# A hybrid attention and mixture-of-experts layer on one core: TensorE's other work within an attention step dealt in three parts instead of two

## The chip, the cores and the metric

One core of a Trainium2 chip runs the whole layer as one program. The metric is the device time of one execution in microseconds (us): here the median of three runs of the kernel before.

## The reference

512 tokens of width 1024, one layer, all in float32. What the attention part computes:

```python
h = rms_norm(x, g_mix)
qa, ka, va, qb, kb, vb, qi, ki, wi, ga, gb = split(h @ w_in)      # 8 heads of 64 for a and b, 8 for the indexer
o_a = softmax(mask_a(rope(qa) rope(ka).T / 8)) @ va               # branch a: block-sparse, causal
score = sum_h wi * relu(rope(qi) . rope(ki))                      # indexer: the 128 best keys of each query
o_b = softmax(mask_topk(rope(qb) rope(kb).T / 8)) @ vb            # branch b: only those keys
x = x + (sigmoid(ga) * (o_a @ w_proj_a) + sigmoid(gb) * (o_b @ w_proj_b)) @ w_out
x = x + hier_moe(rms_norm(x, g_ffn))                              # top group of 4, then 2 of its 8 experts
return rms_norm(x, g_final)
```

## The kernel before, in words

The program has three parts in time. It normalises and transposes x and projects the first chunks of columns; it runs the attention, with the rest of the input projections dealt between its steps; then it applies the output projection, routes the tokens and runs all 32 experts, whose weights come in 192 pieces of 1024 KB.

**Weights of the projections.** Each chunk of 256 columns comes by DMA from SP's queue into `raw` buffers (three of them). ScalarE casts each half to the matmul's format (`split`, line 169: the high part, `wh`), and VectorE (first half) or GpSimd (second half) subtracts it from the raw value (line 170: the low part, `wl`). A projection is a row of groups of three 128x512 matmuls (lines 255 to 257: high by high, high by low, low by high), each group an item of the generator `proj_T`.

**The attention.** `attend(quad, work)` is called for a0, a1, b0 and b1, four heads each. A quad has eight steps: two pairs of heads by four query tiles i of 128 rows, with (i+1)*128 keys each. A step has three pieces.

- `scores`: for each of the two heads two matmuls into one of two score banks (lines 432, 433); VectorE adds the mask and takes the minimum (436), ScalarE takes the exponential (437), VectorE the reciprocal and the scaling (438, 439) into `e`.
- `transposes`: TensorE turns `e` by 128x128 blocks (448), and ScalarE copies the result from PSUM to `pt` (450), one copy for each of the two heads.
- `values`: TensorE multiplies `pt` with v (460). At a pair's last tile ScalarE and VectorE split the result into two parts (464, 465).

Transposes and values are those of the step before the scores'. Between the pieces TensorE is given `work`: the generator `others()`, which holds the remaining projections, the indexer's scores (389, 390, with ScalarE's 391 and VectorE's 393), the gates (line 487 is their tanh on ScalarE) and the merge of branch a (503 to 505). `run(work, cost)` takes items from it until their costs (0.64 for a group of three matmuls) use up the amount due. `SHARE` gives for each quad the amount ahead of its first scores and the amount in a step. What is left over is run behind the quad by `run_to`.

VectorE also carries the search for the top keys (`topk`, lines 402 to 404), which is queued behind a0 and runs on through a1 into b0. The order of TensorE's instructions is the program's own in this part (`manual_schedule`), while a scheduler orders those of the other engines around it. [...]

Of the kernel before, what the change touches and what calls it, by code (L numbers as in the profile page):

```python
# [136 lines left out]
def layer_kernel(ctx: ExitStack, tc: tile.TileContext, xT, x, w_ki, w_ch, w_ab, w_out, g_mix, g_ffnk, g_fin, w_r, b_r,  # L137
# [20 lines left out]
    def t2(shape, dtype=F32, name="t2", tag="r"):  # L158
        return temps[tag][0].tile(shape, dtype, tag=tag, name=name, bufs=temps[tag][1])

    def small(shape, name, dtype=F32):
        return sm.tile(shape, dtype, tag=name, name=name)
# [99 lines left out]
    def run(gen, cost=1e9):  # L262

        due[0] += cost
        while due[0] > 0:
            c = next(gen, None)
            if c is None:
                due[0] = 0.0
            elif isinstance(c, str):
                done.add(c)  # L270
            else:
                due[0] -= c
# [142 lines left out]
    def attend(quad, work):  # L415

        br, n4 = quad[0], int(quad[1])
        qs, (ks, klo), v = Q[quad], K[quad], V[br]
        bias_of = causal if br == "a" else sparse
        oh, ol = oT[br]  # L420
        steps = [(pr, i) for pr in range(2) for i in range(NT)]
        es, pts, ops = {}, {}, {}

        def scores(pr, i):
            n = (i + 1) * P
            nm = max(n, 2 * P)
            es[pr, i] = []
            for s in range(2):
                j = 2 * pr + s
                ps = pa.tile([P, 512], F32, tag="sc", name="ps")  # L430
                q = qs[:, j, i * P:(i + 1) * P]
                pe.matmul(ps[:, :nm], q, ks[:, j, :nm], start=True, stop=False)
                pe.matmul(ps[:, :nm], q, klo[:, j, :nm], start=False, stop=True)
                e = t2([P, T], name="e", tag="e")
                st = small([P, 3], "st")
                dve.tensor_tensor_reduce(e[:, :n], ps[:, :n], bias_of(i), -0.125, 3e38, ALU.add, ALU.min, st[:, 0:1])  # L436
                act.activation(ps[:, :n], e[:, :n], AF.Exp, bias=st[:, 0:1], scale=-1.0, accum_out=st[:, 1:2])  # L437
                dve.reciprocal(st[:, 2:3], st[:, 1:2])
                dve.tensor_scalar(e[:, :n], ps[:, :n], st[:, 2:3], None, ALU.mult)
                es[pr, i].append(e)  # L440

        def transposes(pr, i):
            n = (i + 1) * P
            pts[pr, i] = []
            for e in es.pop((pr, i)):
                tr = pt_.tile([P, 512], F32, tag="tr", name="tr")
                for kt in range(i + 1):
                    pe.transpose(tr[:, kt * P:(kt + 1) * P], e[:, kt * P:(kt + 1) * P], ident)
                pt = t2([P, T], name="pt", tag="p")
                act.copy(pt[:, :n], tr[:, :n])  # L450
                pts[pr, i].append(pt)

        def values(pr, i):
            if i == 0:
                ops[pr] = pb.tile([P, 512], F32, tag="o", name="ops")
            pt = pts.pop((pr, i))
            for kt in range(i + 1):
                for s in range(2):
                    h = 4 * n4 + 2 * pr + s
                    pe.matmul(ops[pr][64 * s:64 * s + 64, i * P:(i + 1) * P], v[:, kt, h * DH:(h + 1) * DH],  # L460
                              pt[s][:, kt * P:(kt + 1) * P], start=kt == 0, stop=kt == i)
            if i == NT - 1:
                o = ops.pop(pr)
                act.copy(oh[:, 2 * n4 + pr], o)
                dve.tensor_tensor(ol[:, 2 * n4 + pr], o, oh[:, 2 * n4 + pr].bitcast(F32), ALU.subtract)

        first, share = SHARE[quad]
        run(work, first)
        for m in range(len(steps) + 1):
            if m < len(steps):  # L470
                scores(*steps[m])
            run(work, share / 2)
            if m > 0:
                transposes(*steps[m - 1])
            run(work, share / 2)
            if m > 0:
                values(*steps[m - 1])
        S.free(qs, ks, klo)


# [69 lines left out]
    def others():  # L550
        yield from qk("qi0")
        yield from together(qk("qi1", "qa1", "ka1"), idx_scores(), RATIO)
        yield "a1"
        yield from v_proj("vb")
        yield from qk("qb0", "kb0")
        yield "b0"
        yield from merge_a()
        S.free(*oT["a"])
        yield from qk("qb1", "kb1")
        yield "b1"  # L560
        yield from gates_b()
        yield "end"

    run(v_proj("va"))
    oT["a"] = pair_of_outputs()
    work = others()
    attend("a0", work)
    run_to(work, "a1")
    attend("a1", work)
    S.free(V["a"])  # L570
    run_to(work, "b0")
    oT["b"] = pair_of_outputs()
    for i in range(1, NT):
        topk(i)
    attend("b0", work)
    x2 = []

# [46 lines left out]
    for n in range(4):  # L624
# [6 lines left out]
        for b in range(2):  # L631
# [9 lines left out]
            m = ma[c // 4][:, c % 4]  # L641
# [500 lines left out]
```

## Time and profile before

| what | value |
|---|---|
| median of three runs | 941.35 us (941.22 to 945.83) |
| the profiled execution | 942.32 us; its span 940.4 us |
| TensorE matmuls (PE) | busy 875.7 us, 93% of the span |
| VectorE (DVE) | busy 433.8 us, 46% |
| ScalarE (ACT) | busy 278.3 us, 30% |
| GpSimd (POOL) | busy 176.5 us, 19% |
| mean granted clock of TensorE | 0.985 of full speed |
| HBM traffic | 241.33 MB read, 259 GB/s over the span |

The span is the profiled execution from its first to its last recorded instruction; the execution's own time is 1.9 us longer. The shares are means over stages with different limits: the attention runs from 66 to 372.6 us of the span, the output projection and the routing follow, and from about 470 us on the expert weights flow. A time in a timeline is counted from the start of the span.

### The profile page before, as it was taken

How to read it: one execution, taken by the hardware profiler on the slowest of the kernel's cores; microseconds unless marked ns; L12 is line 12 of the kernel's file. 1: busy time of each engine (PE TensorE's matmuls, PEld its weight loads, DVE VectorE, ACT ScalarE, POOL GpSimd, SP SyncE). 2: the span in 40 equal slices, each digit the busy share in tenths (PEclk: the TensorE clock that was granted, in tenths of full speed). 3: DMA queues.
4: the chain of work that ended last, by engine and by line, in shares of the span. 5: the costliest groups of instructions: out<-in, count | busy, mean ns of one | idle time of the engine just before them, and what ended most of it. 6: DMA issues, size and time to landing. Idle time of an engine off the chain costs nothing. (4 is left out here: it accounts for less than half of the span.)

```text
span 940.4 us, 15614 instructions
## 1 busy us (share of the span) xinstructions
PE 875.7 (93%) x6436; PEld 517.1 (55%) x6436; DVE 433.8 (46%) x991; ACT 278.3 (30%) x585; POOL 176.5 (19%) x112
## 2 busy tenths in 40 slices
PE   7999999989999999889999999998998989987885
PEld 5897779768777877689834342422423223232221
DVE  4737899998544545941823322231322212213004
ACT  5546654562444544433501000000100000100004
POOL 2495334342214711221200000000000000000003
PEclk9999999999999999899999999999999999999898
DMA  8422112112224223455679999999999999999985
GB/s 330 157 71 67 55 36 90 48 57 77 77 82 180 87 69 112 135 229 228 226 317 421 419 420 421 420 418 422 419 420 420 421 422 419 421 420 419 402 327 217
DMA packets 41118, 244.51 MB, mean 260 GB/s; under 512 B 4944, under 2 KB 5328, under 8 KB 16336
## 3 DMA queue, kind: packets, MB, share of 16 engines
q1 hardware_dynamic: 41040, 243.45, 65.0%
q8 instruction: 52, 0.85, 0.4%
q14 instruction: 26, 0.21, 0.1%
HBM read 241.33 MB, written 2.10 MB: 259 GB/s over the span
## 5 line engine op out<-in xcount | busy, mean ns | idle before, releaser
L860 PE MATMUL h<-we,xs 128*32 128x512 f32 x2048 | 238.4, 601 | 26.3 <-DMA we<-in_w_e_dram 19.4
L860 PEld LDWEIGHTS h<-we,xs 128*32 128x32 f32 x2048 | 59.1, 110 | 180.5 <-issue 117.4
L867 PE MATMUL y<-we,hT 128*32 128x512 f32 x1024 | 116.3, 595 | 5.3 <-DMA we<-in_w_e_dram 5.2
L255 PE MATMUL mm<-xh,wh 128*128 128x512 f32 x272 | 109.9, 404 | 0.8 <-DVE bias L393 0.8
L257 PE MATMUL mm<-xh,wl 128*128 128x512 f32 x272 | 107.5, 395 | 0.0
L256 PE MATMUL mm<-xl,wh 128*128 128x512 f32 x272 | 107.5, 395 | 0.0
L1072 POOL TENSOR_TENSOR fo<-x,gfn 128x512 f32<-128x512 f32 x4 | 5.0, 1282 | 450.0 <-DVE x L927 450.0
L170 POOL TENSOR_TENSOR wl<-raw,wh 128x1024 fp32r<-128x1024 f32 (+1 forms) x23 | 64.5, 2803 | 132.1 <-ACT wh L169 68.5
L927 DVE TENSOR_TENSOR x<-cps,x 128x512 f32<-128x512 f32 x64 | 43.3, 688 | 86.3 <-PE cps L925 86.1
L867 PEld LDWEIGHTS y<-we,hT 128*32 128x32 f32 x1024 | 30.0, 109 | 77.1 <-issue 57.0
L901 DVE SCALAR_TENSOR_TENSOR silu<-silu,gate,h 128x512 f32<-128x512 f32 x16 | 12.0, 747 | 124.5 <-issue 82.8
L257 PEld LDWEIGHTS mm<-xh,wl 128*128 128x128 f32 x272 | 51.1, 188 | 12.6 <-DVE wl L170 0.4
L255 PEld LDWEIGHTS mm<-xh,wh 128*128 128x128 f32 x272 | 51.1, 188 | 11.7 <-issue 1.2
L256 PEld LDWEIGHTS mm<-xl,wh 128*128 128x128 f32 x272 | 51.2, 188 | 9.5
L169 ACT CAST wh<-raw 128x1024 fp32r<-128x1024 f32 (+1 forms) x46 | 45.6, 1028 | 31.9 <-DMA raw<-in_w_ch_dram 13.5
L169 ACT CAST y<-y 128x512 fp32r<-128x512 f32 x32 | 18.8, 586 | 121.7 <-PE y L867 121.7
L908 ACT COPY hT<-htr 128x512 f32<-128x512 f32 x16 | 8.7, 589 | 150.2 <-PE htr L906 150.2
L895 ACT ACTIVATE silu<-h 128x512 f32<-128x512 f32 x16 | 9.6, 598 | 145.1 <-PE h L860 145.1
L170 DVE TENSOR_TENSOR y<-y,y 128x512 fp32r<-128x512 f32 x32 | 22.0, 689 | 62.9 <-ACT y L169 62.8
L437 ACT ACTIVATE ps<-e,st 128x128 f32<-128x128 f32 (+3 forms) x64 | 33.5, 524 | 43.9 <-DVE st L436 43.6
L170 DVE TENSOR_TENSOR wl<-raw,wh 128x1024 fp32r<-128x1024 f32 (+1 forms) x23 | 31.9, 1389 | 26.9 <-ACT wh L169 22.3
L677 PE MATMUL mm<-woh,mt 128*128 128x256 f32 x128 | 37.4, 293 | 0.0
(201 smaller groups left out, 1570.7 us busy)
## 6 DMA issues: line engine op xcount, KB each, us to landing
we<-in_w_e_dram SPq DMA_DIRECT2D x192, 1024.0 KB, 19.8
raw<-in_w_ch_dram SPq DMA_DIRECT2D x44, 512.0 KB, 4.1
raw<-in_w_ab_dram SPq DMA_DIRECT2D x8, 512.0 KB, 4.1
raw<-in_w_out_dram SPq DMA_DIRECT2D x6, 512.0 KB, 4.2
xraw<-in_xT_dram SPq DMA_DIRECT2D x8, 256.0 KB, 5.8
xtok<-in_x_dram SPq DMA_DIRECT2D x4, 512.0 KB, 9.1
x<-in_x_dram SPq DMA_DIRECT2D x4, 512.0 KB, 5.1
out_dram<-fo SPq DMA_DIRECT2D x8, 256.0 KB, 2.3
```

Of the source, the lines that this page charges most:

```text
L169: act.copy(hi, raw)
L170: eng.tensor_tensor(lo, raw, hi.bitcast(F32), ALU.subtract)
L255: pe.matmul(ps, a, xk(k, 0), start=k == 0, stop=False)
L256: pe.matmul(ps, a, xk(k, 1), start=False, stop=False)
L257: pe.matmul(ps, lo[:, k, col:col + P], xk(k, 0), start=False, stop=k == NK - 1)
L437: act.activation(ps[:, :n], e[:, :n], AF.Exp, bias=st[:, 0:1], scale=-1.0, accum_out=st[:, 1:2])
L677: pe.matmul(ps, a, hi[:, k], start=k == 0, stop=False)
L860: pe.matmul(ps[h][CAP * e:CAP * (e + 1)], xs[:, k, h, CAP * e:CAP * (e + 1)], w[:, e * FF:(e + 1) * FF], start=k == 0, stop=k == NK - 1)
L867: pe.matmul(ys[h][CAP * e:CAP * (e + 1)], hT[h][:, k, CAP * e:CAP * (e + 1)], w[:, e * FF:(e + 1) * FF], start=k == 0, stop=k == 3)
L895: act.activation(out[h], h1[h], AF.Silu)
L901: dve.scalar_tensor_tensor(a[h], a[h], gate[:, h:h + 1], h3[h], ALU.mult, ALU.mult)
L927: dve.tensor_tensor(o, ps, o, ALU.add)
```

## The change

In `attend` the work between two scores was dealt in halves: one between the scores and the transposes, one between the transposes and the values. Now it is dealt in thirds, and the last third follows the values. In the ninth round of a quad, which has no scores, the last third isn't run there: it is left to what follows the quad. Two lines longer, the program has every line behind 476 two higher.

```diff
@@ -469,12 +469,14 @@
         for m in range(len(steps) + 1):
             if m < len(steps):
                 scores(*steps[m])
-            run(work, share / 2)
+            run(work, share / 3)
             if m > 0:
                 transposes(*steps[m - 1])
-            run(work, share / 2)
+            run(work, share / 3)
             if m > 0:
                 values(*steps[m - 1])
+            if m < len(steps):
+                run(work, share / 3)
         S.free(qs, ks, klo)
```

**TensorE at the first values of b1.** `tr` is the bank of the transposes, `ops` the accumulator of the values, `mm` that of a projection. Before, nine matmuls of work stand between transposes and values, the last six of which are the first six rows here:

```order
L255 MATMUL mm<-xh_96,wh 128x512
L256 MATMUL mm<-xl_98,wh 128x512
L257 MATMUL mm<-xh_96,wl 128x512
L255 MATMUL mm<-xh_97,wh 128x512
L256 MATMUL mm<-xl_99,wh 128x512
L257 MATMUL mm<-xh_97,wl 128x512
L460 MATMUL ops<-pt,vb_1339 64x128 x2
L432 MATMUL ps<-hikb_35_2999,qb_32_2902 128x384
L433 MATMUL ps<-lokb_36_3000,qb_32_2902 128x384
```

Now:

```order
L460 MATMUL ops<-pt,vb_1349 64x128 x2
L255 MATMUL mm<-xh_96,wh 128x512
L256 MATMUL mm<-xl_98,wh 128x512
L257 MATMUL mm<-xh_96,wl 128x512
L255 MATMUL mm<-xh_97,wh 128x512
L256 MATMUL mm<-xl_99,wh 128x512
L257 MATMUL mm<-xh_97,wl 128x512
L432 MATMUL ps<-hikb_35_2999,qb_34_2918 128x384
L433 MATMUL ps<-lokb_36_3000,qb_34_2918 128x384
```

The values (line 460) moved ahead of six matmuls of work, which now stand between them and the next scores (432).

**ScalarE at the first two steps of b1.** Line 487 is 489 in the changed kernel. Before:

```order
L437 ACTIVATE ps,st<-e,st 128x256
L169 CAST wh<-raw 128x1024 x2
L437 ACTIVATE ps,st<-e,st 128x256
L487 ACTIVATE g<-g 128x512
L450 COPY pt<-tr 128x128 x2
L437 ACTIVATE ps,st<-e,st 128x384 x2
```

Now:

```order
L437 ACTIVATE ps,st<-e,st 128x256
L169 CAST wh<-raw 128x1024 x2
L437 ACTIVATE ps,st<-e,st 128x256
L450 COPY pt<-tr 128x128
L489 ACTIVATE g<-g 128x512
L450 COPY pt<-tr 128x128
L437 ACTIVATE ps,st<-e,st 128x384 x2
```

The tanh of a gate moved from ahead of both copies (450) to between them; the two casts (169) stay ahead of the second exponential.

**ScalarE at the second step of b0.** `wab` is a weight of branch a's output. Before:

```order
L169 CAST wh<-raw 128x1024 x2
L437 ACTIVATE ps,st<-e,st 128x384 x2
L169 CAST wab<-raw 128x1024
L450 COPY pt<-tr 128x256 x2
L487 ACTIVATE g<-g 128x512
```

Now:

```order
L169 CAST wh<-raw 128x1024
L437 ACTIVATE ps,st<-e,st 128x384
L169 CAST wh<-raw 128x1024
L437 ACTIVATE ps,st<-e,st 128x384
L169 CAST wab<-raw 128x1024
L450 COPY pt<-tr 128x256 x2
L489 ACTIVATE g<-g 128x512
```

One of the two exponentials (437) moved in between the two casts of `wh`; the copies still stand behind the cast of `wab`.

## Rows read from the trace of the kernel before

**Rows 1.** Each stretch: start:end, length, busy us by engine, clock, DMA share, GB/s.

```profile
66.00:148.80 82.80, 78.21 (x476) 63.94 (x476) 71.41 (x187) 48.70 (x106) 40.60 (x25) 1.00 0.20 66
148.80:223.00 74.20, 68.76 (x419) 56.02 (x418) 71.73 (x184) 36.93 (x80) 28.14 (x18) 1.00 0.19 64
223.00:317.40 94.40, 94.40 (x487) 74.96 (x486) 50.89 (x116) 41.31 (x82) 29.97 (x14) 1.00 0.29 101
317.40:372.60 55.20, 55.20 (x319) 43.41 (x318) 26.85 (x76) 27.61 (x65) 10.84 (x7) 1.00 0.26 80
...
470.00:926.00 456.00, 423.56 (x3722) 143.75 (x3714) 115.17 (x195) 39.16 (x71) 5.00 (x4) 0.99 0.99 407
```

**Rows 2.** Waits of PE up to 470 us: total us, times, longest us.

```profile
PE ps L432 <- DVE e L439: 5.4, 4, 2.1
PE ips L389 <- DVE bias L393: 3.0, 5, 1.3
```

**Rows 3.** Line 450 (copies): what ended ScalarE's idle time, who waited for them (us, times).

```profile
  PE tr L448: 25.8, 23
  PEld ops L460: 1.1, 3
```

**Rows 4.** Timelines of PE, ACT, PE, b1: a group of work, the last copies and values.

```profile
322.63 0.39 PE L255 MATMUL mm<-xh,wh 128*128 128x512 f32 x1
323.33 0.40 PE L255 MATMUL mm<-xh,wh 128*128 128x512 f32 x1
...
367.05 1.07 ACT L450 COPY pt<-tr 128x512 f32<-128x512 f32 x2 [1.53 <-PE tr L448]
369.43 1.09 PE L460 MATMUL ops<-pt,vb 128*64 128x128 f32 x16
```

**Rows 5.** Timeline of ACT, then of PE, the last values of a1.

```profile
200.98 0.62 ACT L316 CAST hikb<-r 64x512 fp32r<-64x512 f32 x1 [2.86 <-DVE r L285]
...
203.42 1.06 ACT L450 COPY pt<-tr 128x512 f32<-128x512 f32 x2
204.25 1.37 PE L460 MATMUL ops<-pt,va 128*64 128x128 f32 x16
```

**Rows 6.** Timeline of ACT, then of PE, the second values of b0.

```profile
241.74 1.05 ACT L169 CAST wh<-raw 128x1024 fp32r<-128x1024 f32 x1 [1.75 <-DMA raw<-in_w_ch_dram]
...
243.30 0.56 ACT L437 ACTIVATE ps<-e,st 128x384 f32<-128x384 f32 x1
...
244.85 0.63 ACT L450 COPY pt<-tr 128x256 f32<-128x256 f32 x2
247.11 0.66 PE L460 MATMUL ops<-pt,vb 128*64 128x128 f32 x8
```

**Rows 7.** Timeline of ACT, then of PE, the fourth values of b0.

```profile
263.02 1.05 ACT L169 CAST wh<-raw 128x1024 fp32r<-128x1024 f32 x1 [1.73 <-DMA raw<-in_w_ch_dram]
265.13 1.09 PE L460 MATMUL ops<-pt,vb 128*64 128x128 f32 x16
```

**Rows 8.** Timeline of ACT, then of PE, the first values of b1.

```profile
326.02 0.62 ACT L487 ACTIVATE g<-g 128x512 f32<-128x512 f32 x1
326.55 0.41 ACT L450 COPY pt<-tr 128x128 f32<-128x128 f32 x2
327.14 0.44 PE L460 MATMUL ops<-pt,vb 128*64 128x128 f32 x4
```

**Rows 9.** Timelines of POOL, DVE (two places) and PE, second scores of a1.

```profile
150.58 2.40 POOL L170 TENSOR_TENSOR wl<-raw,wh 128x1024 fp32r<-128x1024 f32 x1 [0.37 <-POOL loka L319]
151.05 3.01 DVE L170 TENSOR_TENSOR wl<-raw,wh 128x1024 fp32r<-128x1024 f32 x1
...
186.92 1.21 DVE L170 TENSOR_TENSOR wl<-raw,wh 128x1024 fp32r<-128x1024 f32 x1
155.59 0.35 PE L432 MATMUL ps<-hika,qa 128*128 128x256 f32 x1 [1.82 <-DVE e L439]
```

**Rows 10.** Timeline of SP's queue, after the attention.

```profile
409.36 2.60 SPq L609 DMA_DIRECT2D we<-in_w_e_dram  x5
```


## Prediction

> **What bounds the kernel now.** I read the stretches first, because the attention and what follows it have different limits. [...] From 470 on the DMA engines are 0.99 busy: there the expert weights set the pace.
>
> Second, the waits of TensorE [rows 2]: the score matmul of line 432 waits 4 times for line 439 (VectorE's scaling of an earlier step, which frees the score bank), 5.4 us in all and at most 2.1; the indexer's matmul of line 389 waits 3.0 us in 5 pieces. Third, the copies, the operation between transposes and values: [rows 3] shows that only 1.1 us, in 3 places and on the weight load alone, was ever waited for them. The time from the transposes to the values covers them.
>
> Does a delay in the attention reach the end? The burst of expert weights is issued from 409.36 on [rows 10], behind the attention and the output projection, and from there transfers fill the rest [rows 1]. So I pass a delay of TensorE on one to one (an estimate: nothing in 372 to 470 moves against the attention's end).
>
> **The change part by part.** No instruction is added or dropped: the same matmuls stand in another order, and VectorE's and ScalarE's orders are made anew around it; SP's and GpSimd's stay as they were. A group of three 128x512 matmuls takes 0.70 us (322.63 to 323.33, [rows 4]). One step of b1 had 2.10 us of such work on either side of the transposes; now it has 1.40 before them, 1.40 behind them and 1.40 behind the values. Two consequences:
>
> *Scores to scores.* The distance between a step's scores and the next is the same, so the waits for line 439 [rows 2] stay: 0. What a value matmul frees (the pt buffers, the accumulator) nobody waits for.
>
> *Transposes and values come sooner.* The transposes of step m-1 need the exponentials that the scores of step m already needed, by way of the banks: no wait there, 0. The values need ScalarE's copies, and the cover of the copies shrinks by a third. In an ordinary step of b1 the two copies start at 367.05, as soon as the transposes let them, and take 1.07, while the values start at 369.43 [rows 4]: 1.31 us behind the copies' end. With 0.70 less work between, a cushion of 0.6 is left, and a step waits only where ScalarE has something else ahead of the copies. I went through all 32 steps for that, and three places are left.
>
> *a1's last values.* Before, from the last scores to these values lay 7.0 us of other work, now 5.6, so they are due 1.40 earlier, at 202.85 instead of 204.25. But ScalarE works in order, and four casts of the key stack stand ahead of the two copies both before and now: they begin at 200.98, when VectorE's r is ready, 0.62 each, and the copies run from 203.42 to 204.48 [rows 5]. Already before, the values ran 1.37 us instead of 1.09 ([rows 5] against [rows 7], both of 16 matmuls), held by the second copy. They end no sooner now, with 1.40 us more work left behind them: +1.4 at most, 0 if r comes earlier by as much. VectorE carries two instructions fewer ahead of r there, so I take +1.1, near the top.
>
> *b0's second values.* Due 247.11 - 2 x 1.40 = 244.3. The copies stood behind a cast whose DMA landed at 241.74 and ended at 244.85 + 0.63 = 245.48 [rows 6], 1.2 later. Now one exponential of 0.56 more runs ahead of that cast, so the copies may end at 244.9: +0.6 to +1.2, and 0 if the transfer lands sooner; I take +0.8.
>
> *b0's fourth values.* The copies stood behind a cast that waited for its transfer until 263.02, and the values followed at 265.13 [rows 7]. Now the copies stand ahead of that cast in ScalarE's order: 0. Were they still behind it, the values, due 4.2 us of work behind the scores where it was 6.3, would wait those 2.1.
>
> *b1's first values.* Due 327.14 - 1.40 = 325.74. Two casts, an exponential and the gate's tanh (0.62) stand ahead of the copies, which ended at 326.55 + 0.41 = 326.96 [rows 8]. The new order puts the tanh between the two copies: the last one still ends near 327.0. +1.3, bounds 0 and 1.5.
>
> *a0.* TensorE rests 82.80 - 78.21 = 4.6 us there, waiting for VectorE [rows 1, 2], and small waits for copies would run beside that; the indexer's waits can move a little either way: 0, bounds -0.5 and +0.5.
>
> *The third that falls away at a quad's last step* runs behind the last values instead, unbroken, for the same time: 0. *DMA issues and GpSimd's subtractions*: their order is the same, and the buffers are freed by the same matmuls at the same count of work: 0. *Clock*: in both a stretches the granted clock stayed 1.00 in spite of waits of up to 2.1 us [rows 1, 2], and the new ones are shorter: 0.
>
> Sum: 0 + 1.1 + 0.8 + 0 + 1.3 = **+3.2 us**. The profiled execution took 942.32 us (span 940.4), so 945.52; the median of the runs is 0.97 lower, hence **944.6 us**.
>
> **The rivals.**
>
> *1. The port race of a1's second step flips: 942.8.* VectorE's subtraction of line 170 at 151.05 took 3.01 us where the same at 186.92 took 1.21, and GpSimd's half of the same chunk ran from 150.58 to 152.98 [rows 9]; behind it stood the scalings for which the scores at 155.59 waited 1.82. So 3.01 - 1.21 = 1.80 us belong to who came first. In the new order VectorE has two of the search's instructions fewer ahead of this subtraction and could start at about 150.5, just ahead of GpSimd: then GpSimd is late (nobody waits for it) and the wait goes: 944.6 - 1.8. For it: the order; against: the margin is under 0.2 us. [...]
>
> *2. Slower: ScalarE's order costs a wait at many steps: 947.8.* The cushion of an ordinary step of b1 is 0.6 us (taken for a1 too), one tanh is 0.62 [rows 8] and one cast 1.05 [rows 7]. If a cast slips ahead of the copies at about half of the 14 other steps of these two quads, each waits 1.05 - 0.6 = 0.45: 7 x 0.45 = 3.2 on top of the 3.2: 945.52 + 3.2 - 0.97. It decides at the point where something on ScalarE holds the copies up by more than the 0.6. For it: ScalarE's order changed at several places, and VectorE's products that gate the tanh move against the copies. Against: ScalarE sat idle for the transposes 23 times in the 32 steps [rows 3], so there nothing stood ahead. [...]
>
> *3. It does nothing: 941.4.* The r of a1, the transfer of b0 and the tanh of b1 all come as much earlier as the values. For it: they hang on TensorE's work, in part. Against: the casts wait for transfers.
>
> *4. Faster: the scores' 5.4 us [rows 2] go as well and no new wait comes: 942.32 - 5.4 - 0.97 = 936.0.* Against: VectorE is busy 71.73 of 74.20 us in a1 [rows 1], which leaves 2.5 to win there.
>
> **How the numbers follow.** The forecast gets 0.43, rival 1 0.20, rival 2 0.20, rival 3 0.13, rival 4 0.04. A measurement of this kernel can tell about 0.5%, 4.7 us, from no change: 936.6 to 946.1. Rival 4 is faster (0.04). Rival 2 and the upper bounds of the forecast (0.5 + 1.4 + 1.2 + 2.1 + 1.5 = 6.7, 948.0) are slower: 0.20 + 0.04 = 0.24. All else, 0.72, is the same. The low end is the port race with all terms near their lows (942.32 - 1.8 + 0.4 - 0.97 = 940.0), the high end rival 2: 940.0 to 947.8. That leaves out rival 4 and the tails of rivals 1 and 2, under 0.2.
>
> **What would show it.** Right: in the waits, the copies of line 450 appear with about 3 us on line 460, in a1's end, b0's second and b1's first step, and line 432 keeps some 5 us; TensorE's busy time is unchanged, and the burst of expert weights starts about 3 us later. Rival 1: the subtraction at about 151 takes 1.2, and line 432's waits fall to 3.6. Rival 2: waits for line 450 at more than six steps. Rival 3: none of over 0.3. I am wrong in kind if TensorE's waits in the attention change by less than a microsecond but the burst's start moves, or if the time differs with the burst unmoved: then the end does not hang on the attention as I say.

## The result, and the profile after

The changed kernel takes **951.15 us** (median of 5 runs, 950.77 to 951.2) against 941.35 (5 runs, 938.27 to 945.83): a ratio of 1.0099, interval 1.0073 to 1.0125. It is slower by 9.8 us, where 944.6 was forecast with a range up to 947.8.

Where the time went is read first by stretches, as [rows 1] of before. In the changed kernel (start and end, length, busy us by engine, granted clock, DMA share, GB/s; the cuts lie just ahead of the first scores of a quad; the last two rows are short pieces inside a0):

```profile
66.00:157.40 91.40, 83.19 (x481) 68.01 (x480) 73.45 (x188) 48.62 (x106) 41.39 (x27) 0.94 0.18 62
157.40:230.20 72.80, 69.52 (x418) 56.14 (x418) 70.00 (x183) 36.82 (x80) 26.89 (x16) 1.00 0.19 65
230.20:325.80 95.60, 94.93 (x487) 75.29 (x486) 50.18 (x115) 40.98 (x82) 29.52 (x14) 1.00 0.29 100
98.70:102.30 3.60, 3.60 (x18) 2.87 (x18) 1.97 (x3) 1.72 (x3) 2.18 (x2) 0.53 0.63 234
122.60:129.60 7.00, 6.05 (x20) 4.57 (x21) 4.30 (x13) 2.06 (x4) 2.55 (x2) 0.51 0.44 150
```

The a0 stretch grew from 82.80 to 91.40, and its granted clock, 1.00 before, is 0.94. In the two short pieces it is 0.53 and 0.51. The a1 stretch got shorter, 72.80 for 74.20, and b0 longer, 95.60 for 94.40. From the first scores of each quad in the timelines of both kernels and the start of the burst of expert weights:

| piece, us | before | changed | difference |
|---|---|---|---|
| to the first scores of a0 | 71.20 | 72.16 | +0.96 |
| a0, to the first scores of a1 | 77.69 | 85.30 | **+7.61** |
| a1, to the first scores of b0 | 74.27 | 72.91 | -1.36 |
| b0, to the first scores of b1 | 94.36 | 95.64 | +1.28 |
| b1 and the output projection, to the burst | 91.85 | 92.43 | +0.58 |
| from the burst to the span's end | 531.04 | 530.86 | -0.18 |
| span | 940.4 | 949.3 | +8.9 |

Behind the burst little changes here, so the delay in the attention does reach the end one to one. The first line is the start of the program, which the change doesn't touch; in the ten profiles of this case it lies between 70.98 and 72.16.

The waits of TensorE up to 490 us, the counterpart of [rows 2] (total us, times, longest us):

```profile
PE ips L389 <- DVE bias L393: 6.0, 2, 3.4
PE ops L460 <- ACT pt L450: 2.8, 5, 1.0
PE ps L432 <- DVE e L439: 1.9, 2, 1.5
PE mm L255 <- DVE bias L393: 1.4, 1, 1.4
```

The scores' wait for VectorE fell from 5.4 to 1.9. The copies' wait appeared: 2.8 in five places. And the indexer's wait for line 393 doubled from 3.0 in five pieces to 6.0 in two, with 1.4 more for a projection's bank (0.8 before). The two waits of line 389 stand where the clock falls. The timelines of a0 (start and duration in us) show how:

VectorE in the changed kernel, at the first place and at the second:

```profile
93.56 0.68 DVE L436 CUSTOM_DVE_ANT_0 e<-ps,rc 128x512 f32<-128x512 f32 x1
94.17 2.67 DVE L170 TENSOR_TENSOR wl<-raw,wh 128x1024 fp32r<-128x1024 f32 x1
97.39 0.59 DVE L393 SCALAR_TENSOR_TENSOR bias<-ips,wi,bias 128x384 f32<-128x384 f32 x1
...
119.19 3.16 DVE L170 TENSOR_TENSOR wl<-raw,wh 128x1024 fp32r<-128x1024 f32 x1
```

GpSimd there:

```profile
93.36 2.40 POOL L170 TENSOR_TENSOR wl<-raw,wh 128x1024 fp32r<-128x1024 f32 x1 [5.01 <-PE ips L390]
118.90 2.38 POOL L170 TENSOR_TENSOR wl<-raw,wh 128x1024 fp32r<-128x1024 f32 x1 [4.83 <-ACT ips L391]
```

TensorE, behind the two waits:

```profile
98.03 0.50 PE L389 MATMUL ips<-kst,qi 128*128 128x512 f32 x1 [2.63 <-DVE bias L393]
123.55 0.69 PE L389 MATMUL ips<-kst,qi 128*128 128x384 f32 x1 [3.36 <-DVE bias L393]
124.35 0.63 PE L255 MATMUL mm<-xh,wh 128*128 128x512 f32 x1
124.78 0.63 PE L256 MATMUL mm<-xl,wh 128*128 128x512 f32 x1
```

VectorE's subtraction (line 170, the low half of a weight chunk) starts at 94.17, 0.81 us after GpSimd's on the other half of the same chunk, and takes 2.67 us; the second starts 0.29 us after GpSimd's and takes 3.16. Behind each stands the indexer's sum (393) that frees TensorE's bank, so TensorE rests 2.63 and 3.36 us, and afterwards its matmuls start 0.43 us apart (124.35 to 124.78) where [rows 4] have 0.23. In the kernel before, VectorE came first both times.

VectorE in the kernel before:

```profile
91.79 1.21 DVE L170 TENSOR_TENSOR wl<-raw,wh 128x1024 fp32r<-128x1024 f32 x1
114.45 1.22 DVE L170 TENSOR_TENSOR wl<-raw,wh 128x1024 fp32r<-128x1024 f32 x1
```

GpSimd in the kernel before:

```profile
92.19 3.05 POOL L170 TENSOR_TENSOR wl<-raw,wh 128x1024 fp32r<-128x1024 f32 x1 [4.82 <-ACT wh L169]
114.63 3.26 POOL L170 TENSOR_TENSOR wl<-raw,wh 128x1024 fp32r<-128x1024 f32 x1 [5.47 <-PE ips L390]
```

Its subtractions took 1.21 and 1.22, and GpSimd, 0.40 and 0.18 us behind, took 3.05 and 3.26, for which nobody waited. What turned the order is VectorE's queue: before, the subtraction stood ahead of both mask-and-minimum operations of a step (line 436) at the first place and ahead of the second of them at the other; in the changed kernel it stands behind both at either place.

### The profile page after: what moved, and what is told of

Its sections match the earlier page's. It is cut to its first block, busy times and chain, and to the rows that moved or that the text cites. A ratio compares the mean times of both kernels' runs of the same rounds, so it can differ in the third digit from the quotient of the medians.

```text
span 949.3 us, 15613 instructions
## 1 busy us (share of the span) xinstructions
PE 881.1 (93%) x6436; PEld 521.1 (55%) x6436; DVE 433.2 (46%) x991; ACT 277.7 (29%) x585; POOL 176.0 (19%) x112
## 5 line engine op out<-in xcount | busy, mean ns | idle before, releaser
L255 PE MATMUL mm<-xh,wh 128*128 128x512 f32 x272 | 114.3, 420 | 1.4 <-DVE bias L393 1.4
L170 DVE TENSOR_TENSOR wl<-raw,wh 128x1024 fp32r<-128x1024 f32 (+1 forms) x23 | 34.1, 1481 | 28.4 <-ACT wh L169 22.8
```

The source lines that it names most:

```text
L170: eng.tensor_tensor(lo, raw, hi.bitcast(F32), ALU.subtract)
L255: pe.matmul(ps, a, xk(k, 0), start=k == 0, stop=False)
```

## The experiments

**Theory P (the port).** The change reorders VectorE's queue at two places of a0, so that GpSimd's subtraction starts first and VectorE's takes 2.67 and 3.16 us instead of 1.21 and 1.22; the indexer's sums come late, TensorE waits, and its clock falls. "Port" is only my name, here and in the texts on record, for what is at stake between the two: the traces show which of them starts first and how long each takes, and no run shows a port. **Rivals:** C, the copies in a1, b0 and b1, as forecast; D, the dealing itself, which asks for the indexer's matmuls too soon; O, VectorE's order alone, whichever of the two starts first.

### 1 and 2: thirds in one part of the attention only

Against the changed kernel (the second with `!=`):

```diff
+            third = quad == "a0"
-            run(work, share / 3)
+            run(work, share / (3 if third else 2))
...
-            run(work, share / 3)
+            run(work, share / (3 if third else 2))
...
-            if m < len(steps):
+            if third and m < len(steps):
                 run(work, share / 3)
```

Expected, thirds in a0 alone:

> Thirds in a0 alone, halves in a1, b0 and b1. Theory P (the port): in the changed kernel VectorE's order puts both mask-and-minimum operations ahead of the weight subtraction of two chunks of a0, so GpSimd's half of the chunk starts first, VectorE's half takes 2.7 and 3.2 us instead of 1.2, the indexer's sums stand behind it, TensorE waits 2.6 and 3.4 us and runs some matmuls at half its clock afterwards. All of it lies in a0, so this kernel loses about as much as the full change: the stretch from the first scores of a0 to the first of a1 is near 85 us (77.7 before), the time 948 to 951. Rival C (the copies, my forecast's terms): the loss is spread over a1, b0 and b1; then this one stays within 2 us of the kernel before.

Expected, thirds in the rest:

> Halves in a0, thirds in a1, b0 and b1. Theory P: a0 is as before (VectorE's order there is the old one; first scores of a1 about 77.7 us behind those of a0), a1 gains 0 to 3 us (scores wait less for VectorE), b0 and b1 lose 1 to 2 in waits for the copies: time 939 to 943. Rival C: the loss stays, 946 or more.

Thirds in a0 alone: 947.8 us (9 runs, 940.78 to 949.39), ratio 1.0054, interval 1.0023 to 1.0085, just under the 948 to 951 expected. That speaks against C, which puts the loss in a1, b0 and b1; but the times spread over 8.6 us, and the profiled execution is one of the quickest (940.85).

Its waits on VectorE's line 393:

```profile
PE ips L389 <- DVE bias L393: 6.0, 2, 3.4
PE mm L255 <- DVE bias L393: 1.6, 1, 1.6
```

Its stretches, a0 and the pieces behind the two waits:

```profile
66.00:152.00 86.00, 77.67 (x473) 63.75 (x472) 73.22 (x188) 48.28 (x105) 40.74 (x26) 1.00 0.19 64
96.50:101.00 4.50, 3.81 (x26) 2.92 (x27) 3.60 (x9) 2.30 (x4) 1.72 (x2) 1.00 0.66 233
120.50:127.00 6.50, 5.87 (x31) 4.68 (x32) 6.17 (x21) 2.69 (x5) 2.58 (x2) 1.00 0.52 161
```

The waits are those of the changed kernel, 6.0 and 1.6 for 6.0 and 1.4, and VectorE's two subtractions are as long (2.66 and 3.17 in its timeline). TensorE, VectorE, ScalarE and GpSimd run the same sequence in a0 as in the changed kernel. But the granted clock stayed 1.00, and a0 took 81.25 us instead of 85.30 (near 85 was expected). That splits a0's +7.61, as far as two executions can: the waits are worth 81.25 - 77.69 = 3.6 us, the halved clock 4.05.

In this execution the other pieces more than give the 3.6 us back: against the kernel before, a1 is 1.66 us shorter, the piece from b1 to the burst 2.03 and the one behind the burst 1.38. So no profile shows where the 5 us lie by which the median of 947.8 exceeds that of the kernel before beside it (942.73).

Thirds in the rest: 945.85 us (10 runs, 943.87 to 947.37), ratio 1.0036, interval 1.0013 to 1.006. That is over what I expected (939 to 943), and just under the 946 that C asks for. a0 was as before (77.69), but a1, where I expected a gain, took 77.05 instead of 74.27.

Its a1 and a piece of it, in the stretches:

```profile
148.80:225.80 77.00, 71.45 (x418) 57.56 (x417) 73.69 (x187) 36.99 (x80) 27.57 (x18) 0.98 0.19 62
156.90:161.00 4.10, 4.10 (x24) 3.55 (x23) 4.07 (x16) 1.77 (x7) 0.00 (x0) 0.58 0.39 153
```

TensorE behind a wait just ahead of that piece, in the timeline:

```profile
155.52 0.36 PE L432 MATMUL ps<-hika,qa 128*128 128x256 f32 x1 [1.82 <-DVE e L439]
```

A subtraction of VectorE later in its a1, in the timeline:

```profile
186.48 3.00 DVE L170 TENSOR_TENSOR wl<-raw,wh 128x1024 fp32r<-128x1024 f32 x1
```

The clock fell to 0.58 for some 4 us behind a wait of 1.82 us. The kernel before has the same wait at 155.59 [rows 9], and its clock stayed 1.00. Some 30 us later the subtraction that took 1.21 in [rows 9] took 3.00, with GpSimd ahead of it (from 185.82). The copies waited 0.81 and 0.97 us in this a1 besides.

So the race is not one of a0 alone. At two places of a1, VectorE lost the first and won the second in the kernel before (3.01 and 1.21 us); it won the first and lost the second in the changed kernel (1.22 and 2.50) and with thirds in a0 alone (1.22 and 2.65); it lost both here (2.98 and 3.00). With thirds in a0 alone the second one is followed by a wait of 3.31 us on line 432, and by a clock of 0.50 from 196 to 198.

### 3 and 4: who subtracts

Against the changed kernel; the fourth is made from the kernel before, with `(pool, dve)` in place of `(pool, pool)`. The two chunks are those loaded at the two places.

```diff
-            split(hi[:, a:a + 4], lo[:, a:a + 4], raw, pool if a else dve)
+            split(hi[:, a:a + 4], lo[:, a:a + 4], raw, by[a // 4])
...
-            return load_split(w_ch[CHUNKS.index(name)])
+            by = (pool, pool) if name in ("ka1", "vb0") else (dve, pool)
+            return load_split(w_ch[CHUNKS.index(name)], by=by)
```

Expected, both halves by GpSimd:

> [...] Theory P: the two long waits of line 389 (2.6 and 3.4 us) and the 1.4 us one shrink to under 3 us in all, the granted clock of a0 is 1.00, a0's stretch is 77 to 79 us and the time 941 to 944. Rival D (the dealing itself: with thirds the indexer's matmuls fall due sooner than VectorE can free their banks, whatever else is in its queue): waits of 2 us and more stay at both places and the time stays over 947.

Expected, the halves swapped:

> The kernel before (halves), with the engines of the two chunks (ka1, vb0) swapped: GpSimd subtracts the first half and so starts first, VectorE the second. Theory P: no thirds are needed for the loss; VectorE's subtraction takes 2 to 3.2 us at both places, line 389 waits 2 us or more at one or both, the clock of a0 falls under 1.00 there, a0's stretch is 81 to 86 us, time 945 to 950. Rival D: a0 stays within 1 us of 77.7 and the time within 2 of the kernel before.

The third: 941.37 us (10 runs, 940.21 to 942.23), ratio to the kernel before 0.9994, interval 0.9973 to 1.0014. All of the loss is gone with TensorE's order unchanged, so D falls. (The edit also takes two subtractions off VectorE; experiment 5 leaves them there.)

Its waits (line 390 is the former 389, 394 the former 393, 461 and 451 the former 460 and 450):

```profile
PE ops L461 <- ACT pt L451: 2.8, 5, 1.0
PE ps L433 <- DVE e L440: 1.8, 2, 1.5
PE mm L255 <- DVE bias L394: 1.6, 1, 1.6
PE ips L390 <- DVE bias L394: 0.3, 1, 0.3
```

Its a0, in the stretches:

```profile
66.00:147.00 81.00, 78.28 (x476) 64.22 (x475) 67.80 (x186) 48.21 (x105) 45.84 (x29) 1.00 0.21 70
```

The indexer's 6.0 us are 0.3, the clock is 1.00, a0 takes 75.63 (77 to 79 expected). The copies' 2.8 stay.

The fourth settles little: 942.86 us (10 runs, 939.78 to 943.93), ratio 1.0006, interval 0.9982 to 1.0029, where 945 to 950 was expected. It hardly made the collision that it was meant to make. At the first place GpSimd had the first half from 91.50 to 93.92, and VectorE's half, whose cast comes later, began at 93.89 and took 1.23. At the second place the two met for a moment (GpSimd's row and VectorE's, in the timelines):

```profile
113.97 2.42 POOL L170 TENSOR_TENSOR wl<-raw,wh 128x1024 fp32r<-128x1024 f32 x1 [5.42 <-PE ps L434]
115.85 1.61 DVE L170 TENSOR_TENSOR wl<-raw,wh 128x1024 fp32r<-128x1024 f32 x1
```

GpSimd had 0.54 us left (113.97 + 2.42 - 115.85), VectorE took 1.61 instead of 1.22, and the indexer's wait there was 1.68 instead of 1.28. That fits P, on a small scale.

### 5: who starts first, or VectorE's order alone

VectorE's order in a0 stays that of the changed kernel; GpSimd's half waits for VectorE's. The one-element value is overwritten by the subtraction behind it.

```diff
+            if a and late:
+                pool.tensor_tensor(lo[:, 4, 0:1], raw[:, 0, 0:1], lo[:, 3, 0:1].bitcast(F32), ALU.subtract)
             split(hi[:, a:a + 4], lo[:, a:a + 4], raw, pool if a else dve)
...
+            return load_split(w_ch[CHUNKS.index(name)], late=name in ("ka1", "vb0"))
```

> The changed kernel, with GpSimd's half of the two chunks (ka1, vb0) held back until VectorE's half is done (a one-element subtraction on GpSimd that reads VectorE's result stands ahead of it). VectorE's order in a0 stays that of the changed kernel. Theory P (the port): VectorE's two subtractions take 1.2 us instead of 2.7 and 3.2, line 389's waits fall from 6.0 to 2 to 3 us in all, none over 1.8, the clock of a0 stays 1.00; a0's stretch 77.5 to 80 us (85.3 in the changed kernel), time 942 to 945. Rival O (only VectorE's order counts, not who holds the port): the waits stay at 2.6 and 3.4 and the time at 948 or more.

The result is 943.11 us (10 runs, 941.11 to 944.26), ratio 1.0019, interval 1.0005 to 1.0033: 8 of the 9.8 us come back, and 1.9 remain over the 941.24 of the kernel before beside it.

VectorE's two subtractions and the first sum behind them (line 395 is the former 393), in the timeline:

```profile
93.89 1.22 DVE L170 TENSOR_TENSOR wl<-raw,wh 128x1024 fp32r<-128x1024 f32 x1
95.65 0.60 DVE L395 SCALAR_TENSOR_TENSOR bias<-ips,wi,bias 128x384 f32<-128x384 f32 x1
...
115.89 1.22 DVE L170 TENSOR_TENSOR wl<-raw,wh 128x1024 fp32r<-128x1024 f32 x1
```

GpSimd's one-element operation and its subtraction:

```profile
95.34 0.19 POOL L179 TENSOR_TENSOR wl<-raw,wl 128x1 fp32r<-128x1 f32 x1 [7.29 <-DVE wl L170]
95.61 2.37 POOL L170 TENSOR_TENSOR wl<-raw,wh 128x1024 fp32r<-128x1024 f32 x1
```

The indexer's waits:

```profile
PE ips L391 <- DVE bias L395: 2.6, 2, 1.4
```

a0, in the stretches:

```profile
66.00:147.00 81.00, 76.05 (x456) 62.04 (x455) 67.69 (x181) 48.26 (x105) 39.91 (x28) 1.00 0.21 69
```

In a0 TensorE, VectorE and ScalarE run the same sequence as in the changed kernel. VectorE takes 1.22 instead of 2.67 and 3.16; the waits fall from 6.0 to 2.6, none over 1.4; the clock is 1.00; a0 takes 77.86. O falls, and P stands: what counts at these two places is which of the two subtractions starts first. How much longer the second takes can be estimated from the rows: at 94.17 in the changed kernel VectorE's subtraction took 2.67; GpSimd still had 1.59 to run (93.36 + 2.40 - 94.17), and 1.59 + 1.22 = 2.81 is within 0.2 of it, as if VectorE's 1.22 began only when GpSimd was done. What holds it up no run shows. Not every operation of VectorE takes longer beside GpSimd's subtraction: the mask-and-minimum at 93.56 took 0.68 while that ran, and 0.68 at 130.52 with GpSimd idle.

### 6 and 7: the race taken out of a0 and a1

The edit of experiment 3 with six chunks, `("ka1", "vb0", "vb1", "qb0", "kb0", "ga0")`, in the kernel before (6) and in the changed kernel (7).

Expected, with halves:

> The kernel before (halves), with both halves of six chunks (ka1, vb0, vb1, qb0, kb0, ga0), those of a0 and a1, subtracted by GpSimd. Theory P: line 389 and line 432 wait less, since VectorE has six subtractions of 1.2 to 3 us fewer: 9.2 us of waits fall to 3 to 6, time 2 to 5 us under the kernel before, 937 to 941. If GpSimd's double work makes a chunk late, a wait for its line 170 shows and the time is over 942.

Expected, with thirds:

> The changed kernel (thirds) with both halves of the same six chunks subtracted by GpSimd. Theory P: like the run with two such chunks (941.4) or 1 to 2 us less, 939 to 941.5; the copies' waits of line 460 (2.8 us in the changed kernel) stay, so that it ends over the kernel with halves and the same six chunks by about the 2 to 3 us of these.

With halves: **935.4 us** (4 runs, 934.78 to 935.48), ratio 0.9942, interval 0.9922 to 0.9963, quicker than both kernels and than the 937 to 941 expected. Lines 389 and 432 (390 and 433 in its waits) wait 1.3 and 1.4 us where they waited 3.0 and 5.4:

```profile
PE ps L433 <- DVE e L440: 1.4, 1, 1.4
PE ips L390 <- DVE bias L394: 1.3, 3, 0.7
PE ops L461 <- ACT pt L451: 0.5, 1, 0.5
```

With thirds: 940.13 us (10 runs, 938.72 to 940.83), ratio 0.9991, interval 0.9976 to 1.0006, within the 939 to 941.5 expected. The difference of the two, 4.7 us where 2 to 3 was expected, is the price of the thirds with the race out of a0 and a1. By the starts of the first scores and of the burst in the timelines it lies in a1 (71.82 for 70.37), b0 (95.78 for 94.36), from b1 to the burst (92.03 for 90.75) and behind the burst (0.75); a0 is 0.3 shorter. The copies' waits are 2.8 us for 0.5.

### 8: the same kernel, another execution

> The kernel with thirds in a0 alone once more, for a second profile: its nine times lay between 940.8 and 949.4, and the profiled one (940.85) showed the waits of 6.0 us on line 389 with the granted clock at full speed all through a0. Theory P with the clock: an execution of 946 to 949 shows the same waits (5.8 to 6.2 us) and, behind them, matmuls 0.43 us apart instead of 0.23 with the clock at half, and a0 4 us longer (85 instead of 81.25). If it is a fast one again (under 942), it tells nothing. Rival: the waits themselves differ between executions, by over 2 us.

The result is 942.32 us, one run, between the two cases that I had named, and it tells something: the waits of lines 389 and 255 are again 6.0 and 1.6, so the rival falls, and the clock fell behind the first of the two waits and not behind the second, as the stretches of the two places show:

```profile
96.50:101.00 4.50, 3.72 (x17) 2.58 (x18) 3.41 (x8) 1.71 (x3) 1.28 (x1) 0.62 0.69 233
120.50:127.00 6.50, 4.25 (x24) 3.32 (x25) 6.16 (x17) 2.15 (x4) 2.34 (x2) 1.00 0.51 161
```

Its a0 took 82.76 us. So with the same waits a0 is 81.25 with the clock up throughout, 82.76 with one fall (+1.5) and 85.30 with two, in the changed kernel. The two executions of this kernel differ by 1.47 us in all and by 1.51 in a0. The spread of the nine times is not explained by it: a0's clock is worth 4.05 us at most here and the times lie 8.6 apart, and only one of the nine has a profile.

## Why the prediction was wrong, by its steps

- **a0: "0, bounds -0.5 and +0.5".** This is the step that failed: +7.61 us. I took the indexer's waits as a matter of TensorE's order and priced a small shift. What moved was VectorE's queue, and with it the race of the two subtractions at two places where VectorE had come first by 0.40 and 0.18 us. The race itself stands in my rival 1, but for a1 alone and only as a gain; the same pair of instructions at the other places, where it could be lost, is in no term of the sum.
- **Clock: "the new ones are shorter: 0".** The new waits of a0 are 2.6 and 3.4 us, longer than any of a0 or a1 before (2.1), and the clock fell behind both: 4.05 of the 7.61 us. That a wait of up to 2.1 us is safe was wrong as well: in experiment 2 the clock fell behind one of 1.82. The kernel before had shown a fall, in the stretch behind the attention, which has a wait of 2.8 us for line 170 and a granted clock of 0.91 (its wait, then its stretch):

```profile
PE mm L505 <- DVE wab L170: 2.8, 1, 2.8
372.60:412.00 39.40, 34.54 (x171) 28.64 (x170) 32.06 (x61) 16.64 (x42) 13.28 (x4) 0.91 0.36 120
```

- **Scores to scores: "the waits for line 439 stay: 0".** They fell from 5.4 to 1.9. Rival 1 came true here: VectorE's subtraction in the second step of a1 took 1.22 (at 158.84, 0.28 ahead of GpSimd) instead of 3.01, and the 1.82 us wait went; the one of 2.12 at 192.88 went too, for which no run shows the reason. But a race that was won before was lost, at 191.84 (2.50 for 1.21), so it was not the flip that I had priced alone.
- **The copies: +3.2 in three places.** Right in kind and in these places, as TensorE's timeline of the changed kernel shows (the last values of a1, the second of b0, the first of b1, in two pieces):

```profile
209.87 1.57 PE L460 MATMUL ops<-pt,va 128*64 128x128 f32 x16 [0.97 <-ACT pt L450]
252.25 0.93 PE L460 MATMUL ops<-pt,vb 128*64 128x128 f32 x8 [0.67 <-ACT pt L450]
334.82 0.43 PE L460 MATMUL ops<-pt,vb 128*64 128x128 f32 x2 [0.51 <-ACT pt L450]
335.50 0.43 PE L460 MATMUL ops<-pt,vb 128*64 128x128 f32 x2 [0.25 <-ACT pt L450]
```

  They wait 0.97, 0.67 and 0.76 us before they start, and 0.4 more in a step of a1 that I had not named. Some of the wait is inside the values: 16 matmuls take 1.57 where an undisturbed row in [rows 7] has 1.09, the 8 of b0 0.93 for 0.66 in [rows 6]. The four casts of a1 still stood ahead of the copies, which began at 209.24. The pair of experiments 6 and 7 has +1.45 for a1, +1.43 for b0 and +1.28 from b1 to the burst, where I had 1.1, 0.8 and 1.3.
- **b0's fourth values: 0.** There the values ran 1.42 for 1.09 in the timeline, +0.3.
- **One to one to the end.** Right: the burst of expert weights, 409.36 in [rows 10], starts at 418.44, 9.1 later, and the span ends 8.9 later. It holds to some 2 us only: in experiments 1, 2 and 8 the piece behind the burst is 1.4 to 1.7 us shorter than before; there a wait of TensorE for VectorE just behind the burst's start is 0.2 to 0.3 us instead of 2.6, and why is open.
- **Rival 2** (waits for the copies at many steps) is not what made it slower: five waits in four steps, 2.8 us. It had the time nearest to the result for a wrong reason. My argument against it was weak, though: ScalarE sat idle for the transposes 23 times before [rows 3], and only 5 times, 2.9 us, in the changed kernel.

In all: +3.6 for the waits behind two lost races, +4.05 for the clock behind them, -1.36 in a1, where the scores' shorter waits outweigh the copies, about +1.9 for the copies in b0 and b1, and +0.96 and -0.2 outside.

## What to carry to other kernels

When a change moves one engine's work by hand, read how the scheduler reorders the queues of the others, and look for subtractions on VectorE and GpSimd that start within a microsecond of each other: who is first decided here (in a0 VectorE's took 1.21 and 1.22 us when it was first, 2.67 and 3.16 when GpSimd was), and the loser's queue may be the one TensorE waits for. If it is, take one of the two out of the race (give both halves to the engine nobody waits for, 941.37 us here for 951.15, or hold one back, 943.11) before judging anything else. A wait that grows should be priced with the clock behind it, as a range: in a0 it was from nothing to 4.05 us.

## What was not expected of the hardware

The clock doesn't fall behind every wait of the same length. Behind waits of 2.6 and 3.4 us in a0 (6.0 in all in three profiles, with the same sequence on every engine), it fell twice (0.53 and 0.51 in the short pieces), once (0.62) and not at all (1.00), which is worth 0 to 4.05 us. The profile of the kernel before has waits of 1.82 and 2.12 us in a1 without a fall, and in experiment 2 the clock fell behind that same 1.82. So the length of a wait alone doesn't decide it. No run here shows what does, nor why all five times of the changed kernel lie within 0.5 us (950.77 to 951.2) while those with thirds in a0 alone spread over 8.6, and those of the kernel before beside them over 8.4 (30 runs, 938.37 to 946.75).
